# Loading x in eight blocks of columns, and the gate columns as one 64-column product

## The chip, the cores and the metric

The kernel runs on one core of a Trainium2 chip. The metric is device time in microseconds (us); the figure used is the median of several runs. The engines that matter here are TensorE (PE), VectorE (DVE), ScalarE (ACT), GpSimd (POOL), and SyncE (SP), which issues DMAs. SP, ACT and POOL each feed a DMA queue of their own.

## The reference

One encoder layer on 256 tokens of width 2048, all in float32. Cut to what matters here:

```python
n = rms_norm(h, norm_mix_w)                 # h = x, (256, 2048)
proj = n @ w_in                             # 32 of its columns are the gates a_f, a_b, b_f, b_b
...                                         # gated delta rule, dilated attention
h = h + mixed @ w_out
n = rms_norm(h, norm_ffn_w)
h = h + conv_gated_mlp(n)                   # 2048 -> 2 x 5632 -> 2048
return rms_norm(h, norm_final_w)
```

`rms_norm` multiplies a token's row by the inverse root of its mean square, and each column by a weight.

## The kernel before

Float32 products are made of two float32r parts: every weight tile (`raw`) is split into `hi` (ACT, line 265) and `lo = raw - hi` (DVE, line 266), and n is kept transposed as `xcat`, whose 16 tiles of 128 columns of x hold 256 tokens of the high part and 256 of the low part. A product is hi·hi + hi·lo + lo·hi, three matmuls (lines 314 to 316).

The weights come as 1 MB chunks through SP's queue into four `raw` buffers; `refill` issues as many as have a free buffer. The work on them is a list of items in a fixed order; `run_items` splits up to `LA = 3` items ahead of the one whose matmuls it issues, and after each item lets generators (convolution, gates, attention) issue a bounded amount of their own work. All order on an engine is the order of issue.

Ahead of the first item stands a start-up, which the change is about. Two tiles `xt[0]`, `xt[1]` hold x: the token 4m + 2q + c lies in partition 64c + m of `xt[q]`. Four DMAs on SP's queue load them, each 64 whole rows of 8 KB into 64 partitions (line 349). Behind them stand on the same queue the norm weights `st5`, the 32 gate columns `g_raw`, and the first weight chunks. 34 transposes of the identity (`warm`, line 412) keep PE at work, then one transposes `st5` (line 415). For each `xt[q]`, ACT squares and sums one half of its columns and DVE the other (lines 419, 420), DVE adds up (line 421), POOL takes the power -1/2 (line 422); then ACT scales `xt[0]` (line 424), and DVE and POOL scale `xt[1]` (line 428) into `xs`. ACT and POOL split the gate columns into `g_hi` and `g_lo` (lines 425, 433). Eight steps `k2` follow, each with four transposes on PE (line 457), two ACT and two DVE instructions that write `xcat` (lines 463, 467). From step 3 on the gate matmuls (lines 448 to 450, 48 in all, 32 columns of weights by 256 tokens) are issued between the transposes, the last 18 behind item 0. Two weight splits stand after steps 4 and 7.

Another place in the kernel issues loads whose source has an outermost count of 2, as the changed x loads have (line 837, the rows for the triangular solve, on POOL's queue; `a_d` is in DRAM and `Bt` in SBUF):

```python
src = bass.AP(tensor=a_d.tensor, offset=a_d.offset + r0 * 64, ap=[[0, 2], [4096, 32], [1, (r1 - r0) * 64]])
nc.gpsimd.dma_start(Bt[0:64, r0:r1, :].rearrange("p r c -> p (r c)"), src)
```

Of the kernel before, what the change touches and what calls it, by code (L numbers as in the profile page):

```python
# [4 lines left out]
F32 = mybir.dt.float32  # L5
F32R = mybir.dt.float32r
I32 = mybir.dt.int32
AF = mybir.ActivationFunctionType
ALU = mybir.AluOpType

P = 128
T = 256
D = 2048
KT = D // P
# [4 lines left out]
EPS = 1e-6  # L19
SCALE = 128.0 ** -0.5  # L20
Z0 = 3 * DW
G0 = 4 * DW
# [63 lines left out]
def block_kernel(tc, A, out, dbg=None):  # L86
    nc = tc.nc
# [3 lines left out]
    ACT = nc.scalar.activation  # L91
    V = nc.vector
    G = nc.gpsimd
    mm = nc.tensor.matmul
    stt = V.scalar_tensor_tensor

    w_in, w_out = A["w_in"][0], A["w_out"][0]
    w_up, w_down = A["w_ffn_in"][0], A["w_ffn_out"][0]
    xd = A["x"][0]
# [23 lines left out]
    DB = Slots(banks[2:6])  # L123
# [6 lines left out]
    neghalf = cp.tile([P, 8], F32, name="neghalf")  # L130
    poshalf = cp.tile([P, 8], F32, name="poshalf")
    nw_mix = cp.tile([P, KT], F32, name="nw_mix")
    nw_ffn = cp.tile([P, KT], F32, name="nw_ffn")
    dnw = cp.tile([P, 1], F32, name="dnw")
# [6 lines left out]
    ss = cp.tile([P, 8, 2, H], F32, name="ss")  # L141
# [6 lines left out]
    xcat = xp.tile([P, KT, 512], F32R, name="xcat")  # L148
# [18 lines left out]
    def pump(bv, ba=None):  # L167

        ba = bv if ba is None else ba
        state["v"] = min(state["v"] + bv, bv)  # L170
        state["a"] = min(state["a"] + ba, ba)
        for t in list(gens):
            if state["v"] <= 0 or state["a"] <= 0:
                break
            while True:
                try:
                    c = next(t[2])
                except StopIteration:
                    gens.remove(t)
                    break  # L180
                more = False
                if not isinstance(c, tuple):
                    c = (c, 0)
                elif len(c) == 3:
                    more = True
                state["v"] -= c[0]
                state["a"] -= c[1]
                if not more or state["v"] <= 0:
                    break
# [43 lines left out]
    chunks = []  # L233
# [13 lines left out]

    prog = {"dma": 0, "split": 0, "mm": 0}

    def refill():  # L250
        while prog["dma"] < len(chunks):
            c = prog["dma"]
            if c >= NR and chunks[c - NR].left:
                break
            nc.sync.dma_start(chunks[c].tile, chunks[c].src)
            prog["dma"] += 1

    def split(u):
        it = items[u]
        src = it.view(it.chunk.tile)  # L260
        a, b = src.shape[1], src.shape[2]
        sl = slice(it.at, it.at + a * b)
        hi = his[u % NU][:, sl].rearrange("p (a b) -> p a b", a=a)
        lo = los[u % NU][:, sl].rearrange("p (a b) -> p a b", a=a)
        ACT(hi, src, AF.Copy)  # L265
        V.tensor_sub(lo, src, hi.bitcast(F32))  # L266
        it.hi, it.lo = hi, lo
        it.chunk.left -= 1

    def run_items(upto=None):  # L270

        n = len(items) if upto is None else upto
        pend = state.pop("pend", None)
        while prog["mm"] < n:
            i = prog["mm"]
            while prog["split"] < min(len(items), i + LA + 1):
                split(prog["split"])
                prog["split"] += 1
                refill()
            if pend:  # L280
                pend()
                pend = None
            items[i].mms(items[i].hi, items[i].lo)
            pend = items[i].done
            prog["mm"] += 1
            pump(BV + 100 * (i < 64), BA)
        state["pend"] = pend
# [36 lines left out]
    def evac(out_ap, acc, n=P, perm=None):  # L324

        a = acc[:n, :T]
        if perm:
            a = a.rearrange("p (c m) -> p c m", c=4)
        ACT(out_ap, a, AF.Copy)  # L329

    def natural(ap):

        return ap.rearrange("p (m c) -> p c m", c=4)


    g0_, x0 = pool("xload", side="right")
    xt = [x0.tile([P, D], F32, name=f"xt{i}") for i in range(2)]
    xs = [x0.tile([P, D], F32, name=f"xs{i}") for i in range(2)]
    st5 = x0.tile([P, 128], F32, name="st5")
# [3 lines left out]
    V.memset(poshalf, 0.5)  # L343
    ACT(ss[:, 7, 0, 0:1], neghalf[:, 0:1], AF.Square)
    nc.scalar.dma_start(cst[:, :C_TRI], A["consts"][:, :C_TRI])
    for q in range(2):
        for c in range(2):
            src = bass.AP(tensor=xd.tensor, offset=xd.offset + (2 * q + c) * D, ap=[[4 * D, 64], [1, D]])
            nc.sync.dma_start(xt[q][c * 64 : c * 64 + 64], src)
    nc.sync.dma_start(st5[0:16], A["norm_mix_w"][0].rearrange("(k p) -> k p", p=P))  # L350
    nc.sync.dma_start(st5[16:32], A["norm_ffn_w"][0].rearrange("(k p) -> k p", p=P))
    nc.sync.dma_start(st5[32:33], A["delta_norm_w"])
    g_raw = x0.tile([P, KT, 32], F32, name="g_raw")
    g_hi = x0.tile([P, KT, 32], F32R, name="g_hi")
    g_lo = x0.tile([P, KT, 32], F32R, name="g_lo")
    nc.sync.dma_start(g_raw, w_in[:, G0 : G0 + 32].rearrange("(k p) c -> p k c", p=P))


    hooks = {}
# [39 lines left out]
    for pr in range(4):  # L399
# [4 lines left out]
        for g in range(3):  # L404
            v_slab(B0 + 6 * DW + g * DW + pr * 256, lambda acc, g=g, pr=pr: hooks["v"](g, pr, acc))
    n_in = len(items)
    refill()


    warm = DB.get()  # L410
    for i in range(34):
        nc.tensor.transpose(warm[:, :P], ident, ident)
    DB.put(warm)
    b0 = DB.get()
    nc.tensor.transpose(b0[:, :33], st5[:33], ident[:33, :33])
    hc = [slice(0, 1024), slice(1024, 2048)]
    for q in range(2):
        s1 = [ss[:, 0, q, e : e + 1] for e in range(3)]
        ACT(xs[q][:, hc[0]], xt[q][:, hc[0]], AF.Square, accum_out=s1[0], scale=D ** -0.5)
        stt(xs[q][:, hc[1]], xt[q][:, hc[1]], 1.0 / D, xt[q][:, hc[1]], op0=ALU.mult, op1=ALU.mult, accum_out=s1[1])  # L420
        V.tensor_scalar(s1[2], s1[0], s1[1], EPS, op0=ALU.add, op1=ALU.add)
        G.tensor_tensor(ss[:, 2, q, 0:1], s1[2], neghalf[:, 0:1], op=ALU.pow)
    for hf in range(2):
        ACT(xs[0][:, hc[hf]], xt[0][:, hc[hf]], AF.Copy, scale=ss[:, 2, 0, 0:1])
    ACT(g_hi, g_raw, AF.Copy)
    for c in range(4):
        cs = slice(c * 512, (c + 1) * 512)
        (V if c < 3 else G).tensor_scalar(xs[1][:, cs], xt[1][:, cs], ss[:, 2, 1, 0:1], None, op0=ALU.mult)
        if c == 1:
            V.tensor_copy(nw_mix, b0[:, 0:16])  # L430
            V.tensor_copy(nw_ffn, b0[:, 16:32])
            V.tensor_copy(dnw, b0[:, 32:33])
    G.tensor_sub(g_lo, g_raw, g_hi.bitcast(F32))
    DB.put(b0)
    nc.gpsimd.dma_start(stq[:120], A["conv_qkv_w"][0].rearrange("d (b p) -> (d b) p", p=P))
    for d in range(3):
        nc.gpsimd.dma_start(stf[d][: 2 * FT], A["conv_ffn_w"][0, d].rearrange("(b p) -> b p", p=P))
# [5 lines left out]

    gacc = next_acc()

    def gate_mms(k2):
        for k in (2 * k2, 2 * k2 + 1):
            mm(gacc[:32, :T], lhsT=g_hi[:, k, :], rhs=xcat[:, k, :T], start=k == 0, stop=False)
            mm(gacc[:32, :T], lhsT=g_hi[:, k, :], rhs=xcat[:, k, T:], start=False, stop=False)
            mm(gacc[:32, :T], lhsT=g_lo[:, k, :], rhs=xcat[:, k, :T], start=False, stop=k == KT - 1)  # L450

    for k2 in range(8):
        bk = DB.get()
        for e in range(2):
            k = 2 * k2 + e
            for q in range(2):
                nc.tensor.transpose(bk[:, e * T + q * P : e * T + (q + 1) * P], xs[q][:, k * P : (k + 1) * P], ident)
        if k2 >= 3:
            gate_mms(k2 - 3)
        for e in range(2):  # L460
            k = 2 * k2 + e
            src = bk[:, e * T : (e + 1) * T]
            ACT(xcat[:, k, :T], src, AF.Copy, scale=nw_mix[:, k : k + 1])
        for e in range(2):
            k = 2 * k2 + e
            src = bk[:, e * T : (e + 1) * T]
            stt(xcat[:, k, T:], src, nw_mix[:, k : k + 1], xcat[:, k, :T].bitcast(F32), op0=ALU.mult, op1=ALU.subtract)
        DB.put(bk)
        if k2 in (4, 7):
            split(prog["split"])  # L470
            prog["split"] += 1
    run_items(1)
    for k2 in range(5, 8):
        gate_mms(k2)
    g0_.__exit__(None, None, None)


# [12 lines left out]
    def gate_hook(acc):  # L490
        gg_, gpool = pool("gates", side="right")
        graw = gpool.tile([32, T], F32, name="graw")
        evac(natural(graw), acc, n=32, perm=True)
        spawn(g_gates(graw, gg_, gpool), 0)


# [712 lines left out]
    go, op = None, None  # L1209
# [38 lines left out]
    go, op = pool("outp", side="left")  # L1248
# [95 lines left out]
    for c in range(2):  # L1344
        k0 = FT - 8 + 4 * c
        ch = Chunk(w_down[k0 * P : (k0 + 4) * P, 3 * 512 :].rearrange("(k p) c -> p k c", p=P), (4, 512))
        for u in range(2):
            i = 2 * c + u
# [136 lines left out]
```

## Time and profile before

| | |
|---|---|
| median of 3 runs | 1547.11 us (1544.25 to 1547.69) |
| the profiled execution: its time, its span | 1545.1 us, 1543.3 us |
| PE busy in the span | 1514.2 us (98%) |
| DVE, ACT, POOL busy | 1039.9, 827.9, 164.5 us |
| granted clock of PE, mean | 0.997 |

The profile is of one execution. Its span runs from the first to the last instruction; times below count from the span's start. Where one engine is busy for 98% of the span, the time follows its own work and the few stretches in which it has none.

### The profile page before, as it was taken

How to read it: one execution, taken by the hardware profiler on the slowest of the kernel's cores; microseconds unless marked ns; L12 is line 12 of the kernel's file. 1: busy time of each engine (PE TensorE's matmuls, PEld its weight loads, DVE VectorE, ACT ScalarE, POOL GpSimd, SP SyncE). 2: the span in 40 equal slices, each digit the busy share in tenths (PEclk: the TensorE clock that was granted, in tenths of full speed). 3: DMA queues.
4: the chain of work that ended last, by engine and by line, in shares of the span. 5: the costliest groups of instructions: out<-in, count | busy, mean ns of one | idle time of the engine just before them, and what ended most of it. 6: DMA issues, size and time to landing. Idle time of an engine off the chain costs nothing.

```text
span 1543.3 us, 28173 instructions
## 1 busy us (share of the span) xinstructions
PE 1514.2 (98%) x11531; PEld 1443.4 (94%) x11531; DVE 1039.9 (67%) x1703; ACT 827.9 (54%) x1430; POOL 164.5 (11%) x245
## 2 busy tenths in 40 slices
PE   7999998999999999999999999999999999999997
PEld 7999998999999999997889999999999999888886
DVE  5878976979864666665557767677676676455454
ACT  5598874545555646554555544544544544344342
POOL 3264552000012202100000000000000000000000
PEclk9999999999999999999999999999999999999999
DMA  9656789646558636634765555565655657566552
GB/s 255 219 184 223 233 294 214 203 145 204 183 142 258 206 122 204 199 124 151 272 217 184 173 191 192 172 209 167 198 185 179 203 165 260 197 210 207 191 191 82
DMA packets 247283, 301.20 MB, mean 195 GB/s; under 512 B 10981, under 2 KB 207766, under 8 KB 246770
## 3 DMA queue, kind: packets, MB, share of 16 engines
q1 hardware_dynamic: 235602, 269.81, 54.4%
q0 software_dynamic: 11120, 29.01, 6.1%
q8 instruction: 90, 1.47, 0.4%
q10 hardware_dynamic: 432, 0.59, 0.1%
q14 instruction: 39, 0.32, 0.1%
HBM read 285.69 MB, written 13.65 MB: 194 GB/s over the span
## 4 chain that ended last, share of the span: by engine, by line
PE 91%; DMA 3%; ACT 2%; issue 2%; DVE 1%; POOL 1%; POOLq 0%; SPq 0%; ACTq 0%; DVEq 0%
PE bank L314 19%; PE bank L316 19%; PE bank L315 19%; PE bank L1224 7%; PE bank L1225 7%; PE bank L1226 7%; PE bank L382 3%; PE bank L383 3%; PE bank L384 3%; DMA raw<-in_w_in_dram 1%; PE bank L978 1%; PE bank L1024 1%; ACT hi L265 1%; PE bank L1019 1%; ACT kb L748 1%
## 5 line engine op out<-in xcount | busy, mean ns | idle before, releaser
L266 DVE TENSOR_TENSOR lo<-raw,hi 128x1024 fp32r<-128x1024 f32 x504 | 619.3, 1230 | 399.9 <-ACT hi L265 397.5
L265 ACT ACTIVATE hi<-raw 128x1024 fp32r<-128x1024 f32 x504 | 533.5, 1060 | 548.7 <-PE bank L315 262.5
L314 PE MATMUL bank<-xcat,hi 128*128 128x256 f32 x2688 | 758.4, 282 | 5.4 <-ACT qk L329 5.1
L315 PE MATMUL bank<-xcat,hi 128*128 128x256 f32 x2688 | 751.8, 280 | 0.0
L316 PE MATMUL bank<-xcat,lo 128*128 128x256 f32 x2688 | 751.6, 280 | 0.0
L314 PEld LDWEIGHTS bank<-xcat,hi 128*128 128x128 f32 x2688 | 506.2, 188 | 8.4 <-ACT qk L329 5.5
L315 PEld LDWEIGHTS bank<-xcat,hi 128*128 128x128 f32 x2688 | 512.0, 190 | 0.0
L316 PEld LDWEIGHTS bank<-xcat,lo 128*128 128x128 f32 x2688 | 505.6, 188 | 0.0
L1226 PE MATMUL bank<-hi,gtl 128*128 128x512 f32 x336 | 130.7, 389 | 0.0
L1225 PE MATMUL bank<-lo,gth 128*128 128x512 f32 x336 | 130.7, 389 | 0.0
L1224 PE MATMUL bank<-hi,gth 128*128 128x512 f32 x336 | 130.7, 389 | 0.0
L382 PE MATMUL bank<-hi,xcat 128*128 128x256 f32 x384 | 109.2, 284 | 0.0
L384 PE MATMUL bank<-hi,xcat 128*128 128x256 f32 x384 | 106.9, 278 | 0.0
L383 PE MATMUL bank<-lo,xcat 128*128 128x256 f32 x384 | 106.8, 278 | 0.0
L1224 PEld LDWEIGHTS bank<-hi,gth 128*128 128x128 f32 x336 | 63.1, 188 | 13.2
L1226 PEld LDWEIGHTS bank<-hi,gtl 128*128 128x128 f32 x336 | 63.1, 188 | 13.1
L1225 PEld LDWEIGHTS bank<-lo,gth 128*128 128x128 f32 x336 | 63.1, 188 | 13.0
L382 PEld LDWEIGHTS bank<-hi,xcat 128*128 128x128 f32 x384 | 72.4, 188 | 0.5
L384 PEld LDWEIGHTS bank<-hi,xcat 128*128 128x128 f32 x384 | 72.5, 189 | 0.0
L383 PEld LDWEIGHTS bank<-lo,xcat 128*128 128x128 f32 x384 | 72.3, 188 | 0.0
L1388 DVE SCALAR_TENSOR_TENSOR fy<-fpad,cwf,fy 128x256 f32<-128x256 f32 x132 | 63.4, 480 | 2.3
L1418 POOL DMA_DIRECT2D nfb<-in_norm_final_w_dram x1 | 0.6, 585 | 485.7 <-PE bank L316 485.7
(299 smaller groups left out, 1439.2 us busy)
## 6 DMA issues: line engine op xcount, KB each, us to landing
raw<-in_w_in_dram SPq DMA_DIRECT2D x104, 1024.0 KB, 5.7
raw<-in_w_ffn_in_dram SPq DMA_DIRECT2D x88, 1024.0 KB, 5.2
raw<-in_w_ffn_out_dram SPq DMA_DIRECT2D x44, 1024.0 KB, 5.0
raw<-in_w_out_dram SPq DMA_DIRECT2D x14, 1024.0 KB, 5.1
rec_d<-rec POOLq DMA_DIRECT2D x8, 768.0 KB, 7.1
rr<-rec_d POOLq DMA_DIRECT2D x6, 512.0 KB, 4.7
xt<-in_x_dram SPq DMA_DIRECT2D x4, 512.0 KB, 8.4
gam<-cg_d POOLq DMA_DIRECT2D x8, 256.0 KB, 8.7
```

The source lines that it names most:

```text
L265: ACT(hi, src, AF.Copy)
L266: V.tensor_sub(lo, src, hi.bitcast(F32))
L314: mm(acc, lhsT=hi[:, kk, :], rhs=xcat[:, k, :T], start=k == 0, stop=False)
L315: mm(acc, lhsT=hi[:, kk, :], rhs=xcat[:, k, T:], start=False, stop=False)
L316: mm(acc, lhsT=lo[:, kk, :], rhs=xcat[:, k, :T], start=False, stop=k == KT - 1)
L382: mm(o, lhsT=xh, rhs=hi[:, kk, :], start=k == 0 and t == 0, stop=False, skip_group_check=True)
L383: mm(o, lhsT=xh, rhs=lo[:, kk, :], start=False, stop=False, skip_group_check=True)
L384: mm(o, lhsT=xl, rhs=hi[:, kk, :], start=False, stop=k == KT - 1, skip_group_check=True)
L1224: mm(a[t], lhsT=xh, rhs=hi[:, kk, :], start=st, stop=False)
L1225: mm(a[t], lhsT=xh, rhs=lo[:, kk, :], start=False, stop=False)
L1226: mm(a[t], lhsT=xl, rhs=hi[:, kk, :], start=False, stop=sp_)
L1388: stt(y, pad[:, d : d + T], cwf[:, d, b : b + 1], y, op0=ALU.mult, op1=ALU.add)
```

## The change

x is loaded as eight blocks, 512 columns of one `xt[q]` each, on all 128 partitions: those of `xt[0]` on SP's queue, those of `xt[1]` on ACT's. The source of a block has three dimensions: 2 token offsets, 64 groups of 4 tokens, 512 columns. `st5` goes to POOL's queue; the first two weight chunks are issued ahead of `g_raw`. Four warming transposes fewer are made, and the copies of the norm weights out of PSUM are issued ahead of the sums. ACT squares and sums all of `xt[0]`, DVE all of `xt[1]`, by block; one reduction, one addition and one power follow for both. Scaling goes by block, two blocks ahead of the eight steps, one each after steps 1 and 3. The splits move to steps 3 and 6. The gate columns' hi and lo parts stand side by side as 64 columns, and one matmul per k multiplies them with high and low part of `xcat` at once (512 columns), 16 in all, behind item 0; three instructions add up the quarters (the fourth is not used).

```diff
-    def refill():
-        while prog["dma"] < len(chunks):
+    def refill(upto=None):
+        while prog["dma"] < (upto or len(chunks)):
...
-    for q in range(2):
-        for c in range(2):
-            src = bass.AP(tensor=xd.tensor, offset=xd.offset + (2 * q + c) * D, ap=[[4 * D, 64], [1, D]])
-            nc.sync.dma_start(xt[q][c * 64 : c * 64 + 64], src)
-    nc.sync.dma_start(st5[0:16], A["norm_mix_w"][0].rearrange("(k p) -> k p", p=P))
...
+    xc = [slice(c * 512, (c + 1) * 512) for c in range(4)]
+    for c in range(4):
+        for q in range(2):
+            src = bass.AP(tensor=xd.tensor, offset=xd.offset + 2 * q * D + c * 512, ap=[[D, 2], [4 * D, 64], [1, 512]])
+            (nc.scalar if q else nc.sync).dma_start(xt[q][:, xc[c]], src)
+    nc.gpsimd.dma_start(st5[0:16], A["norm_mix_w"][0].rearrange("(k p) -> k p", p=P))
...
+    refill(2)
+    nc.sync.dma_start(g_raw, w_in[:, G0 : G0 + 32].rearrange("(k p) c -> p k c", p=P))
     refill()
...
-    for i in range(34):
+    for i in range(30):
         nc.tensor.transpose(warm[:, :P], ident, ident)
...
+    V.tensor_copy(nw_mix, b0[:, 0:16])
+    V.tensor_copy(nw_ffn, b0[:, 16:32])
+    V.tensor_copy(dnw, b0[:, 32:33])
+    DB.put(b0)
     for c in range(4):
+        ACT(xs[0][:, xc[c]], xt[0][:, xc[c]], AF.Square, accum_out=ss[:, 0, 0, c : c + 1], scale=D ** -0.5)
+        stt(xs[1][:, xc[c]], xt[1][:, xc[c]], 1.0 / D, xt[1][:, xc[c]], op0=ALU.mult, op1=ALU.mult,
+            accum_out=ss[:, 0, 1, c : c + 1])
+    V.tensor_reduce(out=ss[:, 1, 0:2, 0:1], in_=ss[:, 0, 0:2, 0:4], axis=mybir.AxisListType.X, op=ALU.add)
+    V.tensor_scalar(ss[:, 1, 0:2, 1:2], ss[:, 1, 0:2, 0:1], EPS, None, op0=ALU.add)
+    G.tensor_tensor(ss[:, 2, 0:2, 0], ss[:, 1, 0:2, 1], neghalf[:, 0:2], op=ALU.pow)
+
+    def scale_x(c):
+        ACT(xs[0][:, xc[c]], xt[0][:, xc[c]], AF.Copy, scale=ss[:, 2, 0, 0:1])
+        V.tensor_scalar(xs[1][:, xc[c]], xt[1][:, xc[c]], ss[:, 2, 1, 0:1], None, op0=ALU.mult)
+
+    scale_x(0)
+    scale_x(1)
...
-        if k2 >= 3:
-            gate_mms(k2 - 3)
...
-        if k2 in (4, 7):
+        if k2 in (1, 3):
+            scale_x(k2 // 2 + 2)
+        if k2 in (3, 6):
             split(prog["split"])
             prog["split"] += 1
+        if k2 == 4:
+            ACT(g_hl[:, :, :32], g_raw, AF.Copy)
+            G.tensor_sub(g_hl[:, :, 32:], g_raw, g_hl[:, :, :32].bitcast(F32))
     run_items(1)
-    for k2 in range(5, 8):
-        gate_mms(k2)
+
+    for k in range(KT):
+        mm(gacc[:64, :512], lhsT=g_hl[:, k, :], rhs=xcat[:, k, :], start=k == 0, stop=k == KT - 1)
...
-        evac(natural(graw), acc, n=32, perm=True)
+        gs = gpool.tile([32, T], F32, name="gs")
+        ACT(gs, acc[32:64, :T], AF.Copy)
+        V.tensor_add(gs, acc[:32, T:512], gs)
+        V.tensor_add(natural(graw), acc[:32, :T].rearrange("p (c m) -> p c m", c=4), gs.rearrange("p (c m) -> p c m", c=4))
```

## Rows read from the trace of the kernel before

**Rows 1.** The page: busy time of each engine over the span.
```profile
PE 1514.2 (98%) x11531; PEld 1443.4 (94%) x11531; DVE 1039.9 (67%) x1703; ACT 827.9 (54%) x1430; POOL 164.5 (11%) x245
```

**Rows 2.** PE's waits, whole span: total us, times, longest us.
```profile
PE bank L412 <- DMA cst<-in_consts_dram: 6.5, 1, 6.5
PE bank L314 <- ACT qk L329: 5.1, 2, 3.4
PE bank L900 <- DVE oo L895: 2.5, 2, 2.2
PE bank L415 <- DMA st<-in_norm_ffn_w_dram: 2.0, 1, 2.0
PE bank L994 <- issue: 1.8, 2, 1.6
PE bank L457 <- ACT xs L424: 1.5, 1, 1.5
```

**Rows 3.** Timeline of the start: start us, us, engine, line, instructions, [idle before].
```profile
0.74 2.49 SPq L349 DMA_DIRECT2D xt<-in_x_dram  x4
6.51 5.78 PE L412 MATMUL bank<-cst 128*128 128x128 f32 x34 [6.51 <-DMA cst<-in_consts_dram]
...
13.80 1.06 ACT L419 ACTIVATE xs<-xt 128x1024 f32<-128x1024 f32 x1 [3.72 <-DMA xt<-in_x_dram]
13.81 1.23 DVE L420 SCALAR_TENSOR_TENSOR xs<-xt 128x1024 f32<-128x1024 f32 x1 [3.29 <-DMA xt<-in_x_dram]
...
15.15 0.21 DVE L421 TENSOR_SCALAR ss<-ss 128x1 f32<-128x1 f32 x1
15.45 0.55 POOL L422 TENSOR_TENSOR ss<-ss,neghalf 128x1 f32<-128x1 f32 x1 [4.31 <-DVE ss L421]
16.03 1.32 DVE L428 TENSOR_SCALAR xs<-xt,ss 128x512 f32<-128x512 f32 x2 [0.66 <-POOL ss L422]
```

**Rows 4.** DMA of 2:13 us, while x comes, and 16:22, weights: GB/s, queues.
```profile
DMA packets 1408, 2.29 MB, mean 208 GB/s; under 512 B 991, under 2 KB 1152, under 8 KB 1152
...
DMA packets 2072, 2.09 MB, mean 348 GB/s; under 512 B 32, under 2 KB 2072, under 8 KB 2072
```

**Rows 5.** Timeline of PE, ACT and DVE around items 0 and 1.
```profile
16.57 2.93 PE L457 MATMUL bank<-cst,xs 128*128 128x128 f32 x15 [0.20 <-DVE xs L428]
23.99 0.60 PE L457 MATMUL bank<-cst,xs 128*128 128x128 f32 x4
25.12 0.28 PE L314 MATMUL bank<-xcat,hi 128*128 128x256 f32 x1
27.73 0.11 PEld L448 LDWEIGHTS bank<-xcat,g_hi 128*32 128x32 f32 x1
30.14 0.62 ACT L329 ACTIVATE graw<-bank 32x256 f32<-32x256 f32 x1 [1.83 <-PE bank L450]
```

**Rows 6.** DMA issues of the page: KB each, median us from issue to landing.
```profile
rec_d<-rec POOLq DMA_DIRECT2D x8, 768.0 KB, 7.1
Bt<-a_d POOLq DMA_DIRECT2D x2, 320.0 KB, 20.9
```

**Rows 7.** Second large `Bt` load: issue, landing; POOL's queue in 261:262, 262:263: packets, MB, share.
```profile
241.38 0.68 POOL L837 DMA_DIRECT2D Bt<-a_d  x1
...
Bt<-a_d POOLq DMA_DIRECT2D x1, 320.0 KB, 21.8
...
q0 software_dynamic: 16, 0.04, 28.5%
...
q0 software_dynamic: 10, 0.03, 22.9%
```

**Rows 8.** DMA of 1310:1340 us (weights in 2 KB rows): GB/s in 40 slices, SP's queue.
```profile
GB/s 153 382 393 391 57 0 33 112 322 407 410 115 0 0 139 268 412 410 169 0 0 109 229 412 401 257 0 0 38 238 401 410 298 14 0 22 106 352 407 407
q1 hardware_dynamic: 3100, 6.18, 61.0%
```

**Rows 9.** Lines of 0:31 us by form: count | busy us, mean ns.
```profile
L467 DVE SCALAR_TENSOR_TENSOR xcat<-bank,nw_mix,xcat 128x256 fp32r<-128x256 f32 x16 | 6.5, 477 | 0.6 <-ACT xcat L463 0.6
L463 ACT ACTIVATE xcat<-bank,nw_mix 128x256 fp32r<-128x256 f32 x16 | 6.3, 485 | 0.8 <-PE bank L457 0.8
L265 ACT ACTIVATE hi<-raw 128x1024 fp32r<-128x1024 f32 x5 | 5.1, 1059 | 0.0
L266 DVE TENSOR_TENSOR lo<-raw,hi 128x1024 fp32r<-128x1024 f32 x4 | 4.7, 1220 | 0.1
L425 ACT ACTIVATE g_hi<-g_raw 128x512 fp32r<-128x512 f32 x1 | 0.6, 609 | 0.0
```

**Rows 10.** Timeline of PE, two 512-column matmuls four apart.
```profile
1399.72 0.39 PE L1226 MATMUL bank<-hi,gtl 128*128 128x512 f32 x1
...
1400.63 0.39 PE L1224 MATMUL bank<-hi,gth 128*128 128x512 f32 x1
```

**Rows 11.** Windows of one us: PE, PEld, DVE, ACT, POOL busy, granted clock, DMA share, GB/s.
```profile
17.00:18.00 1.00, 1.00 (x8) 1.00 (x6) 1.00 (x5) 1.00 (x4) 1.00 (x2) 0.59 1.10 347
...
21.00:22.00 1.00, 1.00 (x11) 0.96 (x10) 0.63 (x2) 0.77 (x3) 1.00 (x4) 1.00 1.11 351
```

More of the change, by code (lines that the diff above doesn't have):

```diff
@@ L345, in block_kernel @@
     nc.scalar.dma_start(cst[:, :C_TRI], A["consts"][:, :C_TRI])
-    for q in range(2):
-        for c in range(2):
-            src = bass.AP(tensor=xd.tensor, offset=xd.offset + (2 * q + c) * D, ap=[[4 * D, 64], [1, D]])
-            nc.sync.dma_start(xt[q][c * 64 : c * 64 + 64], src)
-    nc.sync.dma_start(st5[0:16], A["norm_mix_w"][0].rearrange("(k p) -> k p", p=P))
-    nc.sync.dma_start(st5[16:32], A["norm_ffn_w"][0].rearrange("(k p) -> k p", p=P))
-    nc.sync.dma_start(st5[32:33], A["delta_norm_w"])
+    xc = [slice(c * 512, (c + 1) * 512) for c in range(4)]
[4 more added lines that the diff above has]
+    nc.gpsimd.dma_start(st5[0:16], A["norm_mix_w"][0].rearrange("(k p) -> k p", p=P))
+    nc.gpsimd.dma_start(st5[16:32], A["norm_ffn_w"][0].rearrange("(k p) -> k p", p=P))
+    nc.gpsimd.dma_start(st5[32:33], A["delta_norm_w"])
     g_raw = x0.tile([P, KT, 32], F32, name="g_raw")
-    g_hi = x0.tile([P, KT, 32], F32R, name="g_hi")
-    g_lo = x0.tile([P, KT, 32], F32R, name="g_lo")
-    nc.sync.dma_start(g_raw, w_in[:, G0 : G0 + 32].rearrange("(k p) c -> p k c", p=P))
+    g_hl = x0.tile([P, KT, 64], F32R, name="g_hl")
     hooks = {}
@@ L415, in block_kernel @@
     nc.tensor.transpose(b0[:, :33], st5[:33], ident[:33, :33])
[L416 to L425, printed above, removed]
-    for c in range(4):
[L427 to L434, printed above, removed]
+    V.tensor_copy(nw_mix, b0[:, 0:16])
+    V.tensor_copy(nw_ffn, b0[:, 16:32])
+    V.tensor_copy(dnw, b0[:, 32:33])
+    DB.put(b0)
+    for c in range(4):
+        ACT(xs[0][:, xc[c]], xt[0][:, xc[c]], AF.Square, accum_out=ss[:, 0, 0, c : c + 1], scale=D ** -0.5)
[9 more added lines that the diff above has]
+    scale_x(1)
     nc.gpsimd.dma_start(stq[:120], A["conv_qkv_w"][0].rearrange("d (b p) -> (d b) p", p=P))
@@ L444, in block_kernel @@
     gacc = next_acc()
[L446 to L450, printed above, removed]
     for k2 in range(8):
```

## The prediction

> **What bounds the kernel now.** I read the page first: PE is busy for 1514.2 of 1543.3 us, and no other engine for more than 67% [rows 1]. So the time is PE's work plus the stretches in which PE has none, and the list of PE's waits says where those are. The six longest entries add up to 19.4 us; 10.0 us of them (6.5 for the constants, 2.0 for `st5`, 1.5 for the scaled x) lie in the start-up [rows 2]. From the first real matmuls on, the order of work is fixed and PE is nearly always fed: a start-up that ends d us later ends the kernel d us later, and matmuls saved there are worth their pitch, if PE is what they wait for.
>
> The timeline of the start shows what sets it. All of x has landed at 13.80, when ACT and DVE stop waiting and square the second tile; 1.23 us of sums, 0.21 us of addition and 0.55 us of power follow, and at 16.03 the first scaling of `xt[1]` begins [rows 3]. Items follow 9 us later: item 0 begins at about 25.0, the 18 late gate matmuls at 27.73, and item 1 as they end, at about 29.8 (ACT's copy of the gates, which waits for the last one, starts at 30.14) [rows 5]. I count from "x has landed" to "item 1 begins": 29.8 - 13.8 = 16.0 us.
>
> While x comes, the queues move 208 GB/s; weights move 348 GB/s a little later [rows 4]. So x comes slowly, and its landing is the term to look at first.
>
> **The loads of x.** The change removes four loads of 64 whole rows and adds eight of 256 KB, whose source is 2 x 64 x 512 with the 2 outermost. The trace has no such load on SP's or ACT's queue, but it has one shape like it: the `Bt` loads of line 837, outer count 2, 64 partitions. They are far slower than their size: 320 KB take 20.9 us from issue to landing, where 768 KB on the same queue take 7.1 us [rows 6]. The second was issued at 241.38 and landed 21.8 us later, at 263.2; in its last two microseconds POOL's queue held 28.5% and 22.9% of the sixteen engines, 4.6 and 3.7 of them, and moved 0.04 and 0.03 MB in 1 us each [rows 7]. A load spread over all sixteen would not leave three quarters of them alone. Smaller `Bt` loads may be in this share, and SP's weight loads ran beside it, so the rows show few engines and not which number. I read them as such a load being split by its outermost count: two engines for it.
>
> If x's blocks are split so, 2 MiB pass through two engines, 1.049 MB each. What can one engine move in 2 KB rows? At 1310 to 1340 us, where weights come in such rows, SP's queue moves 6.18 MB in 61.0% of 16 engines' 30 us, 292.8 us of engine time: 21.1 GB/s per engine. The best slice has 412 GB/s, 25.7 per engine [rows 8]. So 1.049 MB take 40.8 to 49.7 us. I take 24 GB/s, nearer to the upper end, because two engines do not share the memory with fourteen others: 43.7 us. The first bytes move at about 2.1 us: 2.10 MB of x and 0.07 of constants at 208 GB/s would end at 12.5 from there, and x counts as landed at 13.8, 1.3 us after [rows 3, 4]. So x lands at 2.1 + 43.7 + 1.3 = 47.1 us, 33.3 us later than before.
>
> That takes it that SP's and ACT's blocks go to the same two engines. Both queues are given the same shape and draw on the same sixteen; I hold that likelier than two separate pairs, which is the second rival.
>
> [...]
>
> **What else moves, counted from x landed.**
> The sums: the last block is 512 columns, so ACT's and DVE's last sums are about half of 1.06 and 1.23 us [rows 3], 0.5 us less; a reduction of eight values is new on the path, at about the 0.21 us of the small addition beside it, with a hop 0.3 us. Scaling begins at 2.0 us after landing, where it was 2.23.
> ACT then has until `split(1)` and the last `xcat` parts: four scalings of 512 columns (0.6 us each, as the 0.609 of `g_hi`), sixteen `xcat` at 0.39 us (6.3 / 16), two splits of 1.06 and the gate split of 0.61 [rows 9]: 11.4 us, from 2.0 to 13.4. DVE has four scalings of 0.66 (1.32 / 2) [rows 3], sixteen `xcat` at 0.41 and two `lo` of 1.22 [rows 9]: 11.6 us, and starts on `xcat` a little behind ACT, so it ends at about 14.7. Item 0 needs `xcat` of steps 0 to 3 and the first split, now after step 3: on DVE 4 scalings, 8 `xcat`, one `lo`, with the hand-over 10.2 us after landing, where item 0 was at 11.2. The gate matmuls no longer stand ahead of it.
> Item 0 takes 2.7 us as before, to 12.9. Behind it 16 gate matmuls of 512 columns at 0.23 us (four in 0.91 [rows 10]) take 3.6 us, to 16.5; before, 18 of 0.113 us took 2.05. The last one needs `xcat` of k = 15 at 16.3, later than DVE's 14.7, so they hide it.
> Item 1 begins at 16.5 instead of 16.0. I add 0.5 us for the clock: before, it was granted at 0.59 at 17 us, after PE had stood nearly idle from 12.3 to 16.0, and was back at 1.00 at 21 [rows 11]; transposes went at 0.195 us instead of 0.15 or less [rows 5]. Now PE idles for some 35 us. Ends of this term: 0 and 3 us.
> Costed at nothing: the gate sum, one ACT and two DVE instructions of 256 columns instead of one (about 1.3 us), hidden by item 1's 2.7 us, since item 2 is the first to need that accumulator; without that cover it costs 1.3. `st5` on POOL's queue, the four warming transposes and the earlier copies of the norm weights lie in the long wait for x. The first chunks and `g_raw` stand on SP's queue behind `xt[0]` on the two loaded engines (64 KB of each chunk per engine, 2.7 us at 24 GB/s): chunks 0 and 1 land some 2.7 and 5.4 us after x, `g_raw` by about 8, chunk 2 by 11. First used at 7.8 (split 0), 9.6 (gate split) and 15; bounds 0 and 1 us, I take 0.
>
> **Sum.** 33.3 + 0.5 + 0.5 = 34.3 us. Against the profiled execution's own 1545.1 us (1.8 around its span) that is 1579.4; the median shown is 2.0 above that execution, so 1581 us. By the ends (40.8 to 49.7 us of transfer, -1 to +4 for the rest) 1577 to 1591.
>
> **The rivals.**
> *Spread over sixteen (not slower).* SP's queue may split blocks by their 128 partitions. For it speaks that weight loads on 128 partitions run at 348 GB/s [rows 4]; against it the `Bt` rows. 2.17 MB then take 6.2 us, and x lands near 9.6. But the gain is mostly not had: DVE's sums stand behind the copies of the norm weights, these behind 30 warming transposes, which end at 6.51 + 30/34 x 5.78 = 11.6 [rows 3]; with the transpose of `st5`, three copies and four sums of 0.66 us DVE ends at 14.9 and scaling begins at 16.1, against 16.03. With the 14.5 us from there to item 1 instead of 13.8, 1548; up to 2.5 us less if the constants land earlier than 6.5. 1545 to 1549. It decides if x lands before about 12.
> [...]
> *Two pairs of engines.* SP's and ACT's blocks go to different pairs, as the 3.7 to 4.6 engines of POOL's queue [rows 7], more than one pair, allow: 0.52 MB per engine, 21.8 us, landing at 25.2. 11.4 + 1 later: 1559 to 1560 us.
> *Much slower.* At the rate of the `Bt` loads themselves, 320 KB in 20.9 us [rows 6], x's 2048 KB would take over 60 us with two loads at a time: 1594 us and more. Those loads shared their engines with 1 MB weight loads; x shares them only with itself.
>
> **How the numbers follow.** Same two engines 0.80, two pairs 0.06, spread over sixteen 0.10, still slower 0.04. The prediction is the first case, 1581 us, own range 1573 to 1592. To hold eight in ten with the second case the range is 1557 to 1592; it leaves out the third, the fourth and a little of the first. A change of 0.2%, 3.1 us, is about what a measurement of this kernel can tell from none. Spread over sixteen is the only case near no change: same 0.07, faster 0.03; slower 0.90.
>
> **What would show it.** While x comes, a DMA share of 0.1 to 0.15 and some 48 GB/s, up to about 45 us; ACT and DVE waiting for `xt` four times at about 11 us apart, the last until about 47; PE idle from some 12 us on; item 1 some 17 us after that landing; 16 gate matmuls 0.23 us apart; and from there on the same PE time as before. If x lands by 12 us, or the DMA share is near 1 while it comes, the main step is wrong; if it lands near 25, the pair is.

## The result, and the profile after

The changed kernel takes 1582.0 us (median of 5, 1581.7 to 1585.4), the kernel before 1547.1 in the same comparison (5 runs): 1.0231 times as long, interval 1.0217 to 1.0246, 34.9 us more. The forecast was 1581 us. The profiled execution took 1581.65 us, its span 1579.9.

The page's line of the engines answers to [rows 1]: PE's work is nearly the same (1513.0 against 1514.2 us), its share has fallen, so the 36.6 us that the span grew are idle time.

```profile
PE 1513.0 (96%) x11495; PEld 1440.6 (91%) x11495; DVE 1041.2 (66%) x1710; ACT 828.4 (52%) x1436; POOL 162.8 (10%) x246
```

PE's waits (total us, times, longest) say where. What was 1.5 us for the scaled x in [rows 2] is now one wait of 44.4. The wait for the constants fell from 6.5 to 2.9 us and the one for `st5` from 2.0 to 0.8; the other two shown here are about the size they were.

```profile
PE bank L452 <- ACT xs L431: 44.8, 2, 44.4
PE bank L314 <- ACT qk L329: 4.7, 2, 2.9
PE bank L414 <- DMA cst<-in_consts_dram: 2.9, 1, 2.9
PE bank L902 <- DVE oo L897: 2.5, 2, 2.2
```

The start's timeline answers to [rows 3] and [rows 5]: first the two queues' issues, then DVE, ACT and PE.

```profile
0.74 18.56 SPq L351 DMA_DIRECT2D xt<-in_x_dram  x4
19.35 21.73 SPq L255 DMA_DIRECT2D raw<-in_w_in_dram  x2
2.49 22.68 ACTq L351 DMA_DIRECT2D xt<-in_x_dram  x3
25.21 0.63 ACT L423 ACTIVATE xs<-xt 128x512 f32<-128x512 f32 x1 [22.98 <-issue]
18.32 0.69 DVE L424 SCALAR_TENSOR_TENSOR xs<-xt 128x512 f32<-128x512 f32 x1 [9.01 <-DMA xt<-in_x_dram]
29.01 0.69 DVE L424 SCALAR_TENSOR_TENSOR xs<-xt 128x512 f32<-128x512 f32 x1 [10.00 <-DMA xt<-in_x_dram]
40.45 0.69 DVE L424 SCALAR_TENSOR_TENSOR xs<-xt 128x512 f32<-128x512 f32 x1 [10.73 <-DMA xt<-in_x_dram]
45.89 0.63 ACT L423 ACTIVATE xs<-xt 128x512 f32<-128x512 f32 x1 [10.73 <-DMA xt<-in_x_dram]
50.61 0.69 DVE L424 SCALAR_TENSOR_TENSOR xs<-xt 128x512 f32<-128x512 f32 x1 [9.47 <-DMA xt<-in_x_dram]
52.63 0.88 DVE L432 TENSOR_SCALAR xs<-xt,ss 128x512 f32<-128x512 f32 x2 [0.84 <-POOL ss L428]
53.40 3.98 PE L452 MATMUL bank<-cst,xs 128*128 128x128 f32 x17 [44.45 <-ACT xs L431]
63.88 3.85 PE L473 MATMUL bank<-xcat,g_hl 128*64 128x512 f32 x16
67.57 0.28 PE L314 MATMUL bank<-xcat,hi 128*128 128x256 f32 x1
67.77 0.38 ACT L493 ACTIVATE gs<-bank 32x256 f32<-32x256 f32 x1 [1.63 <-PE bank L473]
```

DVE waits for a block four times, some 10 to 11 us apart; x has landed at 50.6 us, where it was 13.8. Scaling begins 2.0 us later, and item 1 at 67.57, which is 17.0 us after the landing and 37.8 us later than before. Where an engine has waited for a block, its first line after the wait gives the landing, so this view reads a slow load without any view of the queues.

The windows (us; PE, PEld, DVE, ACT, POOL busy, granted clock, DMA share, GB/s) show how the blocks come:

```profile
10.00:20.00 10.00, 0.00 (x0) 0.00 (x0) 0.70 (x2) 0.00 (x0) 0.00 (x0) 0.65 0.13 49
20.00:30.00 10.00, 0.00 (x0) 0.00 (x0) 0.70 (x2) 1.33 (x4) 0.00 (x0) 0.50 0.13 49
30.00:40.00 10.00, 0.00 (x0) 0.00 (x0) 0.00 (x0) 0.72 (x2) 0.00 (x0) 0.50 0.49 137
...
56.00:58.00 2.00, 1.78 (x11) 1.25 (x10) 1.93 (x5) 2.00 (x6) 1.64 (x3) 0.66 1.04 359
58.00:60.00 2.00, 1.19 (x9) 0.77 (x8) 1.77 (x6) 2.00 (x4) 0.00 (x0) 1.00 1.11 366
```

A share of 0.13 is 2.1 of the sixteen engines, and 49 GB/s is 24.5 for each of two. Blocks of both queues are under way from 10 to 30 us: SP's queue has 6.7% of the sixteen engines in that stretch and ACT's 6.4%. Before, the queues moved 208 GB/s while x came [rows 4].

### The profile page after: what moved, and what is told of

Read it like the earlier page. It is cut to its first block, busy times and chain, and to the rows that moved or that the text cites. A ratio compares the mean times of both kernels' runs of the same rounds, so it can differ in the third digit from the quotient of the medians.

```text
span 1579.9 us, 28119 instructions
## 1 busy us (share of the span) xinstructions
PE 1513.0 (96%) x11495; PEld 1440.6 (91%) x11495; DVE 1041.2 (66%) x1710; ACT 828.4 (52%) x1436; POOL 162.8 (10%) x246
## 4 chain that ended last, share of the span: by engine, by line
PE 87%; issue 5%; DMA 3%; ACT 3%; POOL 1%; DVE 1%; POOLq 0%; ACTq 0%; DVEq 0%
PE bank L314 18%; PE bank L316 18%; PE bank L315 17%; PE bank L1226 7%; PE bank L1228 7%; PE bank L1227 7%; PE bank L382 3%; PE bank L383 3%; PE bank L384 3%; DMA raw<-in_w_in_dram 1%; PE bank L980 1%; ACT hi L265 1%; PE bank L1026 1%; DMA u_d<-tm 1%; PE bank L1021 1%
## 5 line engine op out<-in xcount | busy, mean ns | idle before, releaser
L1226 PEld LDWEIGHTS bank<-hi,gth 128*128 128x128 f32 x336 | 63.1, 188 | 12.9
L1226 PE MATMUL bank<-hi,mxh 128*128 128x512 f32 x128 | 50.8, 397 | 0.4 <-DVE hs L1264 0.4
```

The source lines that it names most:

```text
L1226: mm(a[t], lhsT=xh, rhs=hi[:, kk, :], start=st, stop=False)
```

## The experiments

The theory: the 2 x 64 x 512 source puts every block on the same two engines, and nearly all of the 35 us comes from that. Against it stood a second pair of engines for the second queue, the cutting into blocks or the two queues as such, and the gate product with its moved splits. Experiments 1 to 4 ran beside 23 runs of the kernel before (median 1547.24), 5 to 8 beside 21 (1546.77).

**1. The old loads in the changed kernel.** Everything else of the change stays.

```
-    for c in range(4):
-        for q in range(2):
-            src = bass.AP(..., offset=xd.offset + 2*q*D + c*512, ap=[[D, 2], [4*D, 64], [1, 512]])
-            (nc.scalar if q else nc.sync).dma_start(xt[q][:, xc[c]], src)
+    for q in range(2):
+        for c in range(2):
+            src = bass.AP(..., offset=xd.offset + (2*q + c)*D, ap=[[4*D, 64], [1, D]])
+            nc.sync.dma_start(xt[q][c*64 : c*64 + 64], src)
```

> The changed kernel with one part undone: x comes by the four old loads (64 whole rows of 8 KB each, SP's queue); all else as changed. If the outermost count of 2 is the cause (two DMA engines per load): x lands at 13 to 14 us as in the kernel before, item 1 begins some 16.9 us later as measured in the changed kernel (50.6 to 67.5), 30.5 to 31, and the time is 1546 to 1549 us. If the rest of the change carried a good part of the loss (order on DVE, gate product behind item 0, clock), it stays above 1555.

Measured: 1549.31 us, 1.0020 times before (1.0008 to 1.0033). The loads alone carry 32.7 of the 34.9 us. Its timeline:

```profile
13.78 0.69 DVE L424 SCALAR_TENSOR_TENSOR xs<-xt 128x512 f32<-128x512 f32 x1 [0.61 <-DMA xt<-in_x_dram]
...
17.63 0.88 DVE L432 TENSOR_SCALAR xs<-xt,ss 128x512 f32<-128x512 f32 x2 [0.84 <-POOL ss L428]
...
32.48 0.28 PE L314 MATMUL bank<-xcat,hi 128*128 128x256 f32 x1
```

x has landed at 13.78 as before, but item 1 begins at 32.5, some 1.5 to 2 us later than I expected. `xt[1]` lands all at once here, and DVE, which now does all the sums of that tile, needs four of them before scaling can begin at 17.63 (16.03 in [rows 3]). The sums by block pay only where the blocks arrive one by one.

**2. The load's shape alone, in the kernel before.** Two loads of 128 rows of 8 KB with the 2 outermost, on SP's queue; no blocks of columns, no second queue, the old gate matmuls.

```
-        for c in range(2):
-            src = bass.AP(..., offset=xd.offset + (2*q + c)*D, ap=[[4*D, 64], [1, D]])
-            nc.sync.dma_start(xt[q][c*64 : c*64 + 64], src)
+        src = bass.AP(..., offset=xd.offset + 2*q*D, ap=[[D, 2], [4*D, 64], [1, D]])
+        nc.sync.dma_start(xt[q], src)
```

> The kernel before with one part of the change alone: two loads of x, whole rows, source 2 x 64 x 2048 with the 2 outermost, both on SP's queue; no blocks, no second queue, nothing else changed. Two engines per load: 49 GB/s and a DMA share of 0.13 while x comes, x landed at 2.1 + 2.097 MB / 49 GB/s + 0.4 = 45.3 us, 31.5 later than before, time 1577 to 1580 us. If cutting into blocks or the second queue makes the loads slow: x lands at 9 to 14 us and the time stays within 3 us of 1547.

Measured: 1577.64 us, 1.0199 (1.0173 to 1.0226). The timeline of DVE and one window:

```profile
24.70 1.23 DVE L419 SCALAR_TENSOR_TENSOR xs<-xt 128x1024 f32<-128x1024 f32 x1 [23.80 <-DMA xt<-in_x_dram]
...
44.86 1.23 DVE L419 SCALAR_TENSOR_TENSOR xs<-xt 128x1024 f32<-128x1024 f32 x1 [18.60 <-DMA xt<-in_x_dram]
```
```profile
3.00:20.00 17.00, 6.12 (x34) 5.88 (x33) 0.00 (x0) 0.00 (x0) 0.00 (x0) 0.74 0.13 50
```

Share 0.13 and 50 GB/s again, with a quarter as many loads and rows four times as long. The shape is enough; the number of blocks, their width and the second queue are not the cause.

**3. All eight blocks on SP's queue.** If the queues had a pair of engines each, one queue would be half as fast as two.

```
-            (nc.scalar if q else nc.sync).dma_start(xt[q][:, xc[c]], src)
+            nc.sync.dma_start(xt[q][:, xc[c]], src)
```

> The changed kernel with all eight blocks on SP's queue, ahead of the weights on that queue. If the two queues use the same two engines and x landed at 50.6 instead of 47 because 0.26 MB of weights passed these engines ahead of the last blocks: 49 GB/s as with two queues, x landed at 45 to 46 us, time 4 to 5 us below the changed kernel, 1577 to 1578. If the weights were not what stood between: x lands at 50 again and the time stays at 1582. If each queue had a pair of its own, x would come at half the rate and land near 90 us, 1620 or more.

Measured: 1580.43 us, 1.0218 (1.0195 to 1.0240), 1.6 below the changed kernel with intervals that overlap. The blocks land at 9.34, 14.68, 20.03, 25.39, 30.73, 36.08, 42.22 and 48.23 us. Its windows, its queue and its last block:

```profile
3.00:20.00 17.00, 4.96 (x31) 4.64 (x31) 1.02 (x5) 0.72 (x2) 0.00 (x0) 0.78 0.13 48
...
46.00:48.00 2.00, 0.00 (x0) 0.00 (x0) 0.00 (x0) 0.00 (x0) 0.00 (x0) 0.50 1.08 324
```
```profile
0.75 31.48 SPq L351 DMA_DIRECT2D xt<-in_x_dram  x8
32.27 11.92 SPq L255 DMA_DIRECT2D raw<-in_w_in_dram  x2
...
48.23 0.69 DVE L424 SCALAR_TENSOR_TENSOR xs<-xt 128x512 f32<-128x512 f32 x1 [11.45 <-DMA xt<-in_x_dram]
```

One queue moves 48 GB/s where two moved 49: it is one pair for both. Six blocks are 5.35 us apart, 262 KB in that time, 49 GB/s. The last two take 6.1 and 6.0 us, and the weights are issued from 32.27 on. So some of the weights' cost seems to stay even with x ahead of them, which is why the time fell by 1.6 us and not by the 4 to 5 expected; whether it lies in the engines or the memory wasn't told apart.

**4. The same blocks as 128 rows.** Each block is 128 consecutive tokens by 512 columns, so that its outermost count is 128; the tokens' order, which the old source made, is made where the transposes' results are read.

```
-            src = bass.AP(..., offset=xd.offset + 2*q*D + c*512, ap=[[D, 2], [4*D, 64], [1, 512]])
+            src = xd[q*P : (q+1)*P, xc[c]]
...
-            src = bk[:, e*T : (e+1)*T]
-            ACT(xcat[:, k, :T], src, AF.Copy, scale=...)
+            src = natural(bk[:, e*T : (e+1)*T])
+            ACT(by_cm(xcat[:, k, :T]), src, AF.Copy, scale=...)     # ap.rearrange("p (c m) -> p c m", c=4)
```

> The changed kernel with the eight blocks on two queues kept, but the source of each is 128 rows of 512 columns (128 tokens in natural order, outermost count 128); the order of tokens is restored where PSUM is read into xcat. If the outermost count is the cause: DMA share near 1 and 300 GB/s or more while x comes, x landed by 9 to 10 us; the constants land at about 3 to 4 us, so the warming transposes and the copies are done by 9 and hardly hold DVE; item 1 begins at about 27, 3 us before that of the kernel before, time 1543 to 1546. If DVE's sums are held by the copies until 12, as the recorded rival has it: 1545 to 1549. If blocks or two queues are the cause of the slow load: above 1570.

Measured: 1546.52 us, 0.9997 (0.9985 to 1.0010). A window while x comes, and the timeline:

```profile
2.00:4.00 2.00, 0.00 (x0) 0.00 (x0) 0.00 (x0) 0.23 (x2) 0.97 (x2) 1.00 0.91 270
```
```profile
2.60 5.56 SPq L255 DMA_DIRECT2D raw<-in_w_in_dram  x2
10.15 0.17 DVE L418 COPY nw_mix<-bank 128x16 f32<-128x16 f32 x1 [9.23 <-PE bank L417]
13.20 0.69 DVE L424 SCALAR_TENSOR_TENSOR xs<-xt 128x512 f32<-128x512 f32 x1 [0.42 <-DMA xt<-in_x_dram]
```

All 35 us are gone, with the eight blocks, the two queues and the gate product still there. This is what the first rival forecast for a load over sixteen engines, no change, but only in part for its reason. DVE does wait for the copies of the norm weights until 10.15; the last block, though, lands only at 13.20, and not by 10 as I expected. SP's queue is through with its own blocks early and issues the weights from 2.60 on, beside ACT's last two blocks (issued from 3.92 to 5.35); experiment 5 asks whether that is why.

**5. x first in line.** Experiment 4 with all blocks on SP's queue ahead of the weights, and the copies of the norm weights behind DVE's sums.

```
-            (nc.scalar if q else nc.sync).dma_start(xt[q][:, xc[c]], src)
+            nc.sync.dma_start(xt[q][:, xc[c]], src)
...
-    V.tensor_copy(nw_mix, b0[:, 0:16])      # and nw_ffn, dnw, DB.put(b0)
     for c in range(4): ...                  # sums
+    V.tensor_copy(nw_mix, b0[:, 0:16])      # and nw_ffn, dnw, DB.put(b0)
```

> The kernel of e4 (blocks of 128 rows, tokens put in order at the PSUM read) with two edits: all eight blocks on SP's queue ahead of the weights, and the three copies of the norm weights behind the sums. In e4 the last block of ACT's queue landed at 13.2 us though the queues moved 250 to 370 GB/s, and 0.6 us of DVE's wait was for the copies. If the weight chunks on SP's queue took the place of ACT's blocks: x now lands at 9.5 to 10.5, DVE's last sum starts then, scaling begins at 12 to 12.5 (15.2 in e4), item 1 at 27 (30.1), time 2 to 3 us under e4, 1543.5 to 1545. If ACT's queue was late by itself: also earlier, so this run does not part the two, but if x lands at 13 again, the rate of the loads is the limit and the time stays at 1546.5.

Measured: 1542.83 us, 0.9969 (0.9956 to 0.9981): faster than both kernels. Window and timeline:

```profile
2.00:9.00 7.00, 4.89 (x29) 4.89 (x30) 1.59 (x5) 2.40 (x8) 0.97 (x2) 1.00 0.93 303
```
```profile
10.19 0.69 DVE L420 SCALAR_TENSOR_TENSOR xs<-xt 128x512 f32<-128x512 f32 x1 [0.68 <-DMA xt<-in_x_dram]
...
12.20 0.88 DVE L428 TENSOR_SCALAR xs<-xt,ss 128x512 f32<-128x512 f32 x2 [0.62 <-POOL ss L424]
...
27.16 0.28 PE L314 MATMUL bank<-xcat,hi 128*128 128x256 f32 x1
```

While x comes the queues move 303 GB/s. Its last block lands at 10.19, 3.0 us earlier than in experiment 4 and 3.6 earlier than before; item 1 begins 2.6 us earlier than before. Some 4 us are what the idea of the change was worth with another source shape. The last issue of x is over at 4.77 here and at 5.35 on ACT's queue in experiment 4, so ACT's later issue would by itself explain some 0.6 of the 3.0 us; the rest is put down to the weights being behind x, though the run doesn't part the two. Nor does it tell what each of its two edits is worth in time.

**6. More warming transposes on top of 5.** Does the slower clock in the transposes cost anything?

```
-    for i in range(30):
+    for i in range(60):
```

> As e5, with 60 warming transposes instead of 30, so that PE works until about 12 us and is not idle before the first transposes of x. If the low granted clock (0.50 in e4 from 15 to 21 us) delays the eight steps: transposes at 0.11 to 0.15 us instead of 0.23, first write of xcat 0.5 us earlier after scaling begins, item 1 0.5 to 1.5 us earlier than e5. If ACT and DVE set the pace of the steps: item 1 as in e5, and the times agree within their intervals.

Measured: 1544.01 us, 0.9983 (0.9973 to 0.9993), not faster than 5. The window and timeline of this kernel, then the same window of experiment 5's:

```profile
19.00:21.00 2.00, 1.54 (x11) 1.34 (x12) 1.77 (x4) 2.00 (x6) 0.57 (x2) 1.00 1.00 356
```
```profile
12.55 1.34 ACT L427 ACTIVATE xs<-xt,ss 128x512 f32<-128x512 f32 x2 [2.00 <-POOL ss L424]
12.82 0.17 DVE L430 COPY nw_mix<-bank 128x16 f32<-128x16 f32 x1 [1.11 <-PE bank L417]
13.06 0.87 DVE L428 TENSOR_SCALAR xs<-xt,ss 128x512 f32<-128x512 f32 x2
...
27.06 0.28 PE L314 MATMUL bank<-xcat,hi 128*128 128x256 f32 x1
```
```profile
19.00:21.00 2.00, 2.00 (x11) 2.00 (x11) 2.00 (x4) 2.00 (x6) 0.80 (x1) 0.50 1.01 361
```

The granted clock stays at 1.00 where it fell to 0.50 in experiment 5. From ACT's first scaling to item 1 it is 14.5 us here (12.55 to 27.06) and 15.0 in experiment 5 (12.20 to 27.16); from DVE's first scaling it is 14.0 (13.06) against 15.0. So the clock costs this stage some 0.5 to 1.0 us. ACT is busy for 2.0 of 2 us in either window, and DVE for 1.8 and 2.0, which would be why it isn't more. And this gain doesn't reach the time: scaling itself begins 0.35 us later here, as x's last block lands at 10.53 in this execution, and the copies of the norm weights, behind twice as many transposes, hold DVE's scaling to 13.06.

**7. The gate product alone, in the kernel before.** Old loads and sums; the gate columns as one product of 64 columns behind item 0, with its sum.

```
-        if k2 >= 3:
-            gate_mms(k2 - 3)
...
+    for k in range(KT):
+        mm(gacc[:64, :512], lhsT=g_hl[:, k, :], rhs=xcat[:, k, :], start=k == 0, stop=k == KT - 1)
```

> The kernel before with one part of the change alone: the gate columns as one 64-column product behind item 0 (split after step 4, 16 matmuls of 512 columns, sum of the quarters), x loaded and scaled as before. If PE's saved work is what counts (48 matmuls of 0.113 us against 16 of 0.23, 1.7 us): item 1 at 28 us instead of 29.8, time 1545.4. If the place counts, since only 18 of the 48 stood between item 0 and item 1 (2.05 us) and the others in PE's idle time: item 0 about 0.6 us earlier (no gate split ahead of the steps), gate product 3.65 us, item 1 at 30.5 to 31, time 1548 to 1548.5.

Measured: 1545.01 us, 0.9991 (0.9982 to 0.9999). Its timeline:

```profile
27.01 3.85 PE L467 MATMUL bank<-xcat,g_hl 128*64 128x512 f32 x16
...
30.70 0.28 PE L314 MATMUL bank<-xcat,hi 128*128 128x256 f32 x1
```

x landed at 14.26 in this execution, so item 1 comes 16.4 us after it, 0.4 later than before, as its place behind item 0 would have it. The time isn't the 1548 that went with that, though: it is 1.8 us less than before, at the very edge of its interval. So the product costs nothing that shows in the time; what would make up for the 0.4 us, or whether anything is gained, these runs don't settle.

**8. Four outermost instead of two.** The changed kernel with another order of tokens in the tile, undone where the transposes are written. If the number of engines follows the outermost count, x comes twice as fast.

```
-            src = bass.AP(..., offset=xd.offset + 2*q*D + c*512, ap=[[D, 2], [4*D, 64], [1, 512]])
+            src = bass.AP(..., offset=xd.offset + q*P*D + c*512, ap=[[D, 4], [4*D, 32], [1, 512]])
```

> The changed kernel with the source of each block 4 x 32 x 512, the 4 outermost (another order of tokens in the partitions, undone by where the transposes write in PSUM); queues, sizes and order as changed. If the number of DMA engines is the outermost count: DMA share 0.25 and 98 GB/s while only x comes, x landed at 2.1 + 2.097 MB / 98 GB/s + 1.9 = 25.4 us, up to 2 us more beside the weights; time 25 us under the changed kernel, 1557 to 1560. If any outermost count under 16 gives two engines: 49 GB/s and 1582. If this shape is spread over all sixteen: 1546 to 1549.

Measured: 1560.9 us, 1.0094 (1.0077 to 1.0110). Three windows and the last block:

```profile
2.00:4.00 2.00, 1.16 (x6) 1.17 (x7) 0.00 (x0) 0.23 (x2) 0.97 (x2) 1.00 0.34 81
5.00:10.00 5.00, 2.88 (x23) 2.55 (x21) 0.32 (x3) 0.00 (x0) 0.00 (x0) 1.00 0.30 102
4.00:16.00 12.00, 3.88 (x27) 3.55 (x25) 1.02 (x5) 1.33 (x4) 0.00 (x0) 0.85 0.55 151
```
```profile
0.74 3.31 SPq L351 DMA_DIRECT2D xt<-in_x_dram  x4
...
29.54 0.69 DVE L424 SCALAR_TENSOR_TENSOR xs<-xt 128x512 f32<-128x512 f32 x1 [4.19 <-DMA xt<-in_x_dram]
```

Between 5 and 10 us, with the constants landed and few weights moving yet, the share is 0.30 and the rate 102 GB/s, where 0.25 and 98 were expected and an outermost 2 gave 0.13 and 49. DVE's waits end at 12.30, 18.38, 24.65 and 29.54: 5 to 6 us apart where they were 10 to 11. The weights are issued from 4 us on, so the 151 GB/s don't all belong to x; that would also be why the last block lands at 29.5 and not by 27.4 as I expected. The step from two to four takes 21 us off the landing and 21 off the time.

## Why the prediction was right

**The loads.** The step that carried it, few `Bt` engines read as a split by the outermost count, was a leap from [rows 7], whose 4.6 and 3.7 engines give few and not two; the runs show it from four sides: the shape alone brings the loss (2), undoing the loads removes it (1), 128 outermost removes it with the blocks, the queues and the gate product in place (4), and four outermost halve the spacing of the blocks (8). That both queues use the same pair, only held likelier in the forecast, follows from 3: 48 GB/s by one queue, 49 by two.

The share itself says two engines: 0.13, 2.1 of the sixteen, for an outermost 2, with the blocks on two queues as on one (3). Which engines these are, no view names.

**The landing.** Forecast 47.1, measured 50.6. The rate was right: 24 GB/s per engine forecast, 24.5 measured. At 5.35 us a block the eight take 42.8 us, against 43.7; with the first bytes at 2.1, experiment 3's first landing at 9.34 leaves 1.9 for the end, against 1.3. That makes 46.8 us. What was mis-sized is the term of the weights, costed at 0: "the first chunks and `g_raw` stand on SP's queue behind `xt[0]`". So they do, but not behind `xt[1]`, whose blocks are on ACT's queue. SP's queue issues weights from 19.35 on, and by the share they take part of the same two engines while `xt[1]` still comes: of `xt[0]` all has landed at 45.89, and between 46 and 48 us the share is still 0.13, 8.7% of the sixteen engines for ACT's queue and 4.5% for SP's; `xt[1]` needs 4.7 us more. With about half of the pair since 40.45 (ACT's queue has 7.0% of the sixteen engines from 40.5 to 45.8 us and moves 0.12 MB), its last block has some 0.13 MB to go then; alone on the pair, at 49 GB/s, that would take 2.6 us by this estimate. The forecast made only the weights late by that, not x. With all of x ahead of the weights it lands 2.4 us earlier (3); the 1.4 us left there are the last two blocks, slower beside the weights.

**From the landing to item 1.** Forecast 17.0, measured 17.0: scaling 2.0 after the landing (2.0 forecast), the gate product's start at 13.3 (12.9) and 16 matmuls in 3.69 us, 0.231 apart (0.23). The 0.5 us allowed for the clock, granted at 0.50 from 20 to 56 us, 0.66 in 56:58 and 1.00 in 58:60, are of the size of the 0.5 to 1.0 that experiment 6 got back in the same stage.

**What was costed at nothing.** The gate sum: ACT's read begins at 67.77, after item 1 has begun at 67.57, and no wait of PE for it is in the list; hidden, as forecast. The place behind item 0 costs no time that can be measured (7).

**The sum.** The landing's 36.8 us and 1.0 behind it make 37.8 us at item 1. The profiled execution grew by 36.6, the medians by 34.9. PE's waits later on vary from one execution to the next: that for `qk` is 5.1 us before, 4.7 after and 7.7 in experiment 1, and nothing of the change touches it. So the forecast's 34.3 came as near to the medians as it did partly by luck: 3.5 us too little for the landing met such differences. The mechanism is right to about 3 us, not to 1.

**The rivals.** Two pairs of engines fell with the 49 GB/s and experiment 3; "much slower" with the 24.5 GB/s per engine: what made the `Bt` loads slower still, the weight loads beside them or something else, no run tests. The rival of sixteen engines was right about a kernel with another source shape: 1545 to 1549 forecast, 1546.5 measured (4).

## What to carry to other kernels

Before a load is reshaped to come in blocks, look at its outermost count: here 2, 4 and 128 outermost gave blocks that landed some 5.3, 2.9 and 0.9 us apart (the last two from DVE's first to its last block, six blocks, with weights beside them: 12.30 to 29.54 and 4.86 to 10.19), and 2 MiB through two engines cost 35 us. If the tile needs another order of rows, make it where data are copied anyway, as at the read of the transposes' results. Keep all of what the start waits for on the queue that issues the next large loads, ahead of them: with half of x on another queue, beside the weights, x landed at 13.2 us, with all of it ahead of them at 10.2.

## What the hardware showed that I had not expected

A load that has few engines can hold whoever issues it, or the next load behind it. SP's eight issues take 31.48 us in experiment 3 and its four take 18.56 in the changed kernel, where four with an outermost 4 take 3.31 (8). In experiment 2 the two loads of x are issued in 1.32 us, but the 8 KB load behind them is held for 18.61. ACT issues three blocks in 22.68 us, and its first sum runs at 25.21 with "issue" as what it waited for, though in experiment 3 the first block lands at 9.34. It cost nothing here, because the last block decides; an engine with work of its own would have lost it.

Weight chunks, which fill all sixteen engines in the kernel before (a share of 1.10 in [rows 11]), aren't free of it either: one issued behind these blocks needs 32.3 us from issue to landing, where the page has a median of 5.8 for the chunks of `w_in`. Between 36 and 42 us the share is down to 0.16 (54 GB/s) though chunks are still under way, which fits part of each standing behind x on the two loaded engines; no view shows single engines.

Loads of 128 rows on 128 partitions move 303 GB/s (5), the old ones of 64 rows on 64 partitions 208 [rows 4]. What makes the difference isn't shown: the loads of 128 rows share their stretch with weights, and no run here changed the partitions alone.
